# Attention values laid out as [high | low]: two products per part, halves added in SBUF

## The chip, the cores and the metric

The kernel runs on one core of a Trainium2 chip. The metric is the device time of one execution in microseconds. Engines are named as in the profile: PE is TensorE, DVE is VectorE, ACT is ScalarE, POOL is GpSimd, and SP issues most of the loads.

## The reference

Two layers of a decoder trunk over 256 tokens of width 1024. A layer is a feed-forward half-step, a mixer, and a second feed-forward half-step, each between two RMS norms. The mixer runs three branches on one combined projection and merges them by gates:

```
x = x + 0.5 * rms_norm(swiglu(rms_norm(x), w_in, w_out))          # ffn1, ffn2 alike
u, bg, cg, q, kv, nsa_g, q_mem, merge_g = split(h @ w_in)         # mixer
y_conv = bg * short_conv(cg * u, conv_w)                          # width 3
y_nsa  = g0 * (compressed) + g1 * (selected blocks) + g2 * (window)   # 8 heads of 64 in 2 groups
y_mem  = softmax(q_m k_m) v_m                                     # 256 memory tokens, 4 heads of 128
merged = sum_i sigmoid(G_i) * (y_i @ w_branch_i);  x = x + rms_norm(merged @ w_out)
```

The sparse attention ("nsa") has three parts. The compressed part attends to blocks of 32 tokens, each made into one key and one value by a small network with a GELU. With 256 tokens there are four blocks of 64, and all are selected, so the selected part and the window part are both causal attention over all tokens, with keys and values of their own. Each head's three outputs are weighted by gates of the token.

## The kernel before

The 256 tokens are two streams of 128 (t = 0 and 1). Values are kept in fp32 and multiplied as pairs: each operand is split into a high half, a cast to fp32r (on ACT), and a low half, the remainder (a subtraction on DVE), and a product is three matmuls, high by high, low by high and high by low (`mm3`, L336). Weights come by DMA from SP as `raw` tiles of 128x1024 (four buffers, RAWBUFS), and `split_unit` (L276) makes `whi` on ACT and `wlo` on DVE from them (eight buffers each, WBUFS).

The Python program is a loop of steps. A stream yields after each piece of a product; `later(n, fn)` (L326) puts work off by n steps; `background` (L1165) runs up to four lanes of attention tasks beside the streams' products, and new tasks of the kinds "nsa" and "memory" start at least nine steps apart (PACE). The program runs once dry, which records when each weight is asked for, and once for real. Each engine then works through its own list in order; SP's list is that of the loads. The order in the lists, with the waits for data and for free buffers, is all that sets the time.

PSUM has six banks for products (`bank`, L151) and two for transposes (`tbank`, L154). Tiles of 128x520 in SBUF (`ttile`) share eight buffers (TBUFS).

In the mixer of a stream (L1184) the columns of the projection come in this order: keys and values (`kv_first` L692, `kv_second` L735), queries (`q_part` L762), memory queries, the convolution's u, c and b (`conv_part` L1104, `conv_out` L1132), then the gates and branches. Evacuated pieces are turned by TensorE transposes some steps later, which `later` decides: the rotated keys `kd` after three steps (L760), the queries `qe` after two and four, the convolution's input `v` and its gate `bs` after two.

Attention: probabilities `p` go through a turn by DVE (`blocks`), two DMAs on POOL's queue and a split into `turnhi` and `turnlo`, and `attend_values` (L819) multiplies them with the values. The values `vz` of a stream hold, for each kind and group, 128 columns for the high half and 128 for the low one, in which the group's 64 columns are filled and the others are zero; so both groups add up in one bank `o` per stream (`accumulate`, L884), three products per part, and the compressed attention (`cmp_attention`, L1000) adds its product to the same bank. The chain of a bank is closed after three parts (t = 0) or five (t = 1), CHAINS, and then evacuated and split into `ynsa`. The compressed attention is queued as the last of the "nsa" tasks.

Of the kernel before, what the change touches and what calls it, by code (L numbers as in the profile page):

```python
# [28 lines left out]
P = 128  # L29
# [27 lines left out]
CMP = 4  # L57
ATT_A, ATT_B, ATT_C, ATT_D, ATT_T = 1, 3, 2, 5, 10
CHAINS = 3, 5
EARLY, RAMP, SCALES, STAGED = 6, 10, 5, 8  # L60
# [71 lines left out]
def program(tc, nc, pools, a, out, plan):  # L132
# [29 lines left out]


    x = [consts.tile([P, D], F32, name=f"x{t}") for t in range(2)]
    idle = ttile("idle", F32R)
# [377 lines left out]


    dmask = consts.tile([P, P], F32, name="dmask")
    cmadd = consts.tile([P, 2, 16], F32, name="cmadd")
# [5 lines left out]
    smallT = consts.tile([P, 96], F32, name="smallT")  # L552
    vz = [consts.tile([P, 1024], F32R, name=f"vz{t}") for t in range(2)]

    def setup():
# [15 lines left out]
        nc.vector.tensor_reduce(gmask, view(bmask, 0, [[1, 2], [2, 4]]), axis=AX.X, op=OP.add)  # L571
        for t in range(2):
            nc.gpsimd.memset(f32(vz[t]), 0.0)

# [48 lines left out]
    def begin_layer(l):  # L623
        if l == 0:
            with tc.issue_after(latest[0].ins):
                setup()
        S = shared[l] = {"ymem": None, "ynsa": [None] * 2, "o": [None] * 2, "parts": [0, 0],
                         "om": [None] * 2, "mparts": 0, "KC": None,
                         "kd": [None] * 2, "gt": [None] * 2, "QT": [None] * 2, "qm": [None] * 2}
        add(("mem", l), memory(l))  # L630
# [61 lines left out]
    def kv_first(t, l, ps, r):  # L692
        S = shared[l]
        if t == 0:
            S["G"] = [ttile(f"G{i}") for i in range(2)]
            S["KT"] = (gtile("KTh", F32R), gtile("KTl", F32R))
        kvs = ttile("kvs")
        v = kvs[:, 0:384].rearrange("p (x c) -> p x c", x=2)
        src = ps[:, 0:256].rearrange("p (x c) -> p x c", x=2)
        nc.scalar.activation(v[:, :, 0:128], src, AF.Copy, scale=r[0])  # L700
        nc.vector.tensor_scalar(v[:, :, 128:192], src[:, :, 0:64], r[0], None, op0=OP.mult)
        kd = ttile("kd")
        S["kd"][t] = kd
        dup_in(kd, 0, ps, 256, r)
        vpad(t, 0, ps, 384, r)

        def turn():
            pt = tbank()
            for i in range(2):
                nc.tensor.transpose(pt[:, i * 256:i * 256 + P], kvs[:, i * 192:i * 192 + 128], ident)  # L710
                nc.tensor.transpose(pt[:, i * 256 + P:i * 256 + 2 * P], kvs[:, i * 192 + 64:i * 192 + 192], ident)
            for i in range(2):
                G = S["G"][i]
                for half in range(2):
                    col = t * P + 1 - half
                    pr = slice(64 * half, 64 * half + 64)
                    for g in range(2):
                        which = g if half == 0 else 1 - g
                        eng = nc.scalar.copy
                        eng(G[pr, g * 260 + col:g * 260 + col + P],  # L720
                            pt[pr, i * 256 + which * P:i * 256 + (which + 1) * P])

        later(2, turn)
# [5 lines left out]
    def vpad(t, var, ps, c0, r):  # L729
        hi = view(vz[t], var * 512, [[192, 2], [1, 64]])  # L730
        lo = view(vz[t], var * 512 + 256, [[192, 2], [1, 64]])
        src = view(ps, c0, [[64, 2], [1, 64]])
        evac_split(hi, lo, src, r[0])

    def kv_second(t, l, ps, r):  # L735
# [23 lines left out]

        later(3, turn)  # L760

    def q_part(t, l, ps, r):  # L762
# [31 lines left out]

        later(2, turn(0))
        later(4, turn(1))

    def recip_gate(sums, n, gate):
# [5 lines left out]
        return r  # L804

    def values(t, var, g):
        c = var * 512 + g * 128
        return vz[t][:, c:c + 128], vz[t][:, c + 256:c + 384]

# [8 lines left out]

    def attend_values(t, l, parts):  # L819

        def put(hi, lo):
            def go():
                for n, (half, kt, var, g) in enumerate(parts):
                    ph, pl = [v[:, half * 512:(half + 1) * 512] for v in (hi, lo)]
                    c = var * 512 + g * 128
# [3 lines left out]
        return put  # L829

    def nsa_first(l, g):
# [25 lines left out]
        yield ATT_C  # L857
        turn_beside(p, 1024, attend_values(0, l, [(var, 0, var, g) for var in range(2)]), ATT_T)

    def nsa_second(l, var, g):  # L860
# [20 lines left out]
        yield ATT_C  # L881
        turn_beside(p, 1024, attend_values(1, l, [(kt, kt, var, g) for kt in range(2)]), ATT_T)

    def accumulate(t, l, share, products):  # L884
        S = shared[l]
        first = S["o"][t] is None
        if first:
            S["o"][t] = bank("o")
        o = S["o"][t]
        S["parts"][t] += share  # L890
        closing = S["parts"][t] == CHAINS[t]
        for n, (st, mv) in enumerate(products):
            nc.tensor.matmul(o, lhsT=st, rhs=mv, start=(first and (n == 0)),  # L893
                             stop=(closing and n == len(products) - 1), skip_group_check=True)
        if closing:
            y = gtile("ynsa", F32R)
            evac_split(y[:, 0:512], y[:, 512:1024], o)
            S["ynsa"][t] = y

    def compress(l, i):  # L900
# [20 lines left out]
        for u in range(4):  # L921
# [8 lines left out]
            yield 1  # L930
        zc = ttile("zc")
        nc.scalar.copy(zc[0:64, 0:256], z[0:64, 0:256])
        yield 1
        zt = tbank()
        for ht in range(2):
            nc.tensor.transpose(zt[:, ht * 64:(ht + 1) * 64], zc[0:64, ht * P:(ht + 1) * P], ident[0:64, 0:64])
        zv = zt[:, 0:128].rearrange("p (h n) -> p h n", h=2)
        zs = sp.tile([P, 2, 32], F32, name="zs")
# [30 lines left out]
        else:  # L969
# [27 lines left out]
            for tt in range(2):  # L997
                add(("nsa", l, tt), cmp_attention(tt, l))

    def cmp_attention(t, l):  # L1000
# [22 lines left out]
        nc.scalar.copy(view(pc, 32, [[96, 4], [32, 2], [1, 32]]), view(pc, 0, [[96, 4], [0, 2], [1, 32]]))  # L1023
        yield ATT_B
        pt = tbank()
# [5 lines left out]
        yield ATT_D  # L1031
        accumulate(t, l, 1, [(S["VST"][0:96], ph[0:96, :512])])

# [70 lines left out]
    def conv_part(t, l, u_s, c_ps, r):  # L1104
# [23 lines left out]

        later(2, turn)
        return cT  # L1130

    def conv_out(cT, b_ps, r, put):  # L1132
        bs = ttile("bs")
        nc.scalar.activation(bs[:, :512], b_ps, AF.Copy, scale=r[0])

        def turn():
            pt = transpose4(bs, 0)
            nc.vector.tensor_tensor(cT[:, :512], cT[:, :512], pt, op=OP.mult)
            y = gtile("yconv", F32R)
# [4 lines left out]
        later(2, turn)  # L1144

# [183 lines left out]
```

## Time and profile before

| | us |
|---|---|
| runs of the kernel | 1270.59, 1272.78, 1275.57; median 1272.78 |
| profiled execution | 1271.95 |
| span of its trace | 1270.2 |
| PE busy, DVE busy, ACT busy, POOL busy | 1255.8, 895.3, 723.0, 204.3 |

The span is that of the trace; the execution's own time has 1.75 us around it. Busy times of PE are made of printed durations that overlap: a product of 128x512 prints 0.39 us and the next one starts 0.23 us after it. A row of the timeline is: start, duration, engine, line, operation, output <- inputs, and in brackets the idle time before it and what ended that.

### The profile page before, as it was taken

To read this page: it belongs to the slowest core of one execution; us is meant where nothing else is said; L and a number is where in the kernel's file an instruction comes from. 1 tells how busy PE (TensorE), PEld (TensorE's weight loads), DVE (VectorE), ACT (ScalarE), POOL (GpSimd) and SP (SyncE) were. 2 spreads that over 40 slices of the span, in tenths; PEclk is the share of its full clock that TensorE was granted. 3 is DMA by queue.
4 is the path that set the end of the run, shared out by engine and by line. 5 is a ranking of instruction groups with operands and counts; after the bars stand their busy time and mean duration, and the time that the engine had idled before them with its cause. 6 is when DMAs were issued, how large, how long until landed. Compare 5 with 4: busy or idle time off the path is not lost.

```text
span 1270.2 us, 16756 instructions
## 1 busy us (share of the span) xinstructions
PE 1255.8 (99%) x5866; PEld 1037.8 (82%) x5866; DVE 895.3 (70%) x1136; ACT 723.0 (57%) x1123; POOL 204.3 (16%) x404
## 2 busy tenths in 40 slices
PE   9999999999999999999999999999999999999998
PEld 6888888888888788888888888878888888888886
DVE  7767657778887676676576676677798766766753
ACT  5545545877775564454464545568778654545441
POOL 3001600302210010111011013013022100110110
PEclk9999999999999999999999999999999999999999
DMA  7878875776876657787757788748587757577772
GB/s 252 261 246 254 283 255 163 221 229 197 254 247 198 198 170 216 246 262 225 249 174 233 227 269 299 238 146 247 170 259 243 216 178 232 177 233 226 244 249 80
DMA packets 133220, 284.77 MB, mean 224 GB/s; under 512 B 11696, under 2 KB 30800, under 8 KB 133136
## 3 DMA queue, kind: packets, MB, share of 16 engines
q1 hardware_dynamic: 118256, 239.30, 60.4%
q0 software_dynamic: 14848, 44.39, 10.9%
q8 instruction: 46, 0.75, 0.2%
q14 instruction: 38, 0.31, 0.1%
q10 hardware_dynamic: 32, 0.01, 0.0%
HBM read 260.59 MB, written 23.07 MB: 223 GB/s over the span
## 4 chain that ended last, share of the span: by engine, by line
PE 89%; ACT 4%; DVE 3%; DMA 2%; issue 2%; POOL 1%; DVEq 0%; POOLq 0%; ACTq 0%
PE acc L349 34%; PE acc L339 8%; PE acc L337 8%; PE acc L338 8%; PE y L339 7%; PE y L338 7%; PE y L337 7%; PE pt L381 2%; PE br L337 2%; PE br L339 2%; PE br L338 2%; PE o L893 1%; ACT whi L281 1%; DVE wlo L282 1%; DMA raw<-in_cmp_v_w_dram 1%
## 5 line engine op out<-in xcount | busy, mean ns | idle before, releaser
L282 DVE TENSOR_TENSOR wlo<-raw,whi 128x1024 fp32r<-128x1024 f32 (+1 forms) x440 | 532.4, 1214 | 265.4 <-ACT whi L281 261.1
L281 ACT CAST whi<-raw 128x1024 fp32r<-128x1024 f32 (+1 forms) x440 | 458.3, 1046 | 380.2 <-PE acc L349 175.5
L349 PE MATMUL acc<-wlo,hThi 128*128 128x512 f32 x640 | 198.6, 390 | 0.1
L349 PE MATMUL acc<-whi,hThi 128*128 128x512 f32 x640 | 197.7, 390 | 0.8 <-ACT whi L281 0.8
L349 PE MATMUL acc<-whi,hTlo 128*128 128x512 f32 x640 | 197.2, 389 | 0.0
L337 PE MATMUL acc<-whi,hThi 128*128 128x512 f32 (+1 forms) x480 | 187.5, 391 | 0.4 <-ACT hThi L455 0.4
L338 PE MATMUL acc<-wlo,hThi 128*128 128x512 f32 (+1 forms) x480 | 184.9, 385 | 0.0
L339 PE MATMUL acc<-whi,hTlo 128*128 128x512 f32 (+1 forms) x480 | 184.7, 385 | 0.2
L396 POOL DMA_DIRECT2D there<-blocks x176 | 97.0, 557 | 431.7 <-DVE blocks L391 393.0
L349 PEld LDWEIGHTS acc<-wlo,hThi 128*128 128x128 f32 x640 | 120.0, 188 | 25.7 <-DVE wlo L282 0.9
L349 PEld LDWEIGHTS acc<-whi,hThi 128*128 128x128 f32 x640 | 119.6, 188 | 26.1 <-ACT whi L281 1.2
L349 PEld LDWEIGHTS acc<-whi,hTlo 128*128 128x128 f32 x640 | 120.0, 188 | 25.4 <-DVE hTlo L456 0.4
L339 PE MATMUL y<-whi,turnlo 128*128 128x512 f32 x352 | 137.3, 390 | 0.0
L338 PE MATMUL y<-wlo,turnhi 128*128 128x512 f32 x352 | 137.3, 390 | 0.0
L337 PE MATMUL y<-whi,turnhi 128*128 128x512 f32 x352 | 137.1, 389 | 0.0
L339 PEld LDWEIGHTS acc<-whi,hTlo 128*128 128x128 f32 x480 | 90.1, 188 | 18.4 <-DVE hTlo L456 0.6
L337 PEld LDWEIGHTS acc<-whi,hThi 128*128 128x128 f32 x480 | 90.3, 188 | 17.2 <-ACT hThi L455 1.3
L338 PEld LDWEIGHTS acc<-wlo,hThi 128*128 128x128 f32 x480 | 90.4, 188 | 15.3
L337 PEld LDWEIGHTS y<-whi,turnhi 128*128 128x128 f32 x352 | 66.1, 188 | 13.7
L339 PEld LDWEIGHTS y<-whi,turnlo 128*128 128x128 f32 x352 | 66.1, 188 | 13.7
L338 PEld LDWEIGHTS y<-wlo,turnhi 128*128 128x128 f32 x352 | 66.1, 188 | 13.6
L432 POOL TENSOR_TENSOR nr<-nv,mhalf 128x1 f32<-128x1 f32 x28 | 16.7, 597 | 358.0 <-DVE nv L429 357.6
(297 smaller groups left out, 1485.9 us busy)
## 6 DMA issues: line engine op xcount, KB each, us to landing
raw<-in_ffn_w_in_dram SPq DMA_DIRECT2D x160, 512.0 KB, 4.9
raw<-in_w_mix_in_dram SPq DMA_DIRECT2D x96, 512.0 KB, 4.5
raw<-in_ffn_w_out_dram SPq DMA_DIRECT2D x88, 512.0 KB, 4.5
there<-blocks POOLq DMA_DIRECT2D x144, 128.0 KB, 4.3
moved<-there POOLq DMA_DIRECT2D x36, 512.0 KB, 5.5
raw<-in_ffn_w_in_dram SPq DMA_DIRECT2D x32, 256.0 KB, 4.2
raw<-in_w_mem_kv_dram SPq DMA_DIRECT2D x16, 512.0 KB, 4.8
raw<-in_w_mix_out_dram SPq DMA_DIRECT2D x16, 512.0 KB, 4.4
```

The source lines that it names most:

```text
L281: pinned(nc.scalar.copy(hi[:, :n], raw[:, :n]))
L282: pinned(nc.vector.tensor_sub(lo[:, :n], raw[:, :n], f32(hi[:, :n])))
L337: nc.tensor.matmul(ps, lhsT=xh, rhs=wh, start=start, stop=False, skip_group_check=skip)
L338: nc.tensor.matmul(ps, lhsT=xh, rhs=wl, start=False, stop=False, skip_group_check=skip)
L339: nc.tensor.matmul(ps, lhsT=xl, rhs=wh, start=False, stop=stop, skip_group_check=skip)
L349: pinned(nc.tensor.matmul(p[:, :n], lhsT=hT[x2][:, k], rhs=w[:, j * n:(j + 1) * n], start=(k == 0 and i == 0), stop=(k == 7 and i == 2)))
L381: pinned(nc.tensor.transpose(pt[:, j * P:(j + 1) * P], src[:, c0 + j * P:c0 + (j + 1) * P], ident))
L396: nc.gpsimd.dma_start(there[:, q * f:(q + 1) * f].rearrange("(p j) f -> j p f", j=32), blocks[q * 32:(q + 1) * 32, :n].rearrange("j (p f) ...
L432: nc.gpsimd.tensor_tensor(r, v, mhalf, op=OP.pow)
L893: nc.tensor.matmul(o, lhsT=st, rhs=mv, start=(first and (n == 0)), stop=(closing and n == len(products) - 1), skip_group_check=True)
```

## The change

The values of a group become 128 columns, [high | low], 64 each. One product of the high probabilities with all 128 columns gives high by high in the bank's upper 64 rows and high by low in its lower 64; a second one, with the 64 high columns, adds low by high to the upper rows. The halves, the groups and the compressed part are then added in an SBUF tile `yf` by `gather`: ACT copies the compressed part's bank `oc`, DVE adds each half of each group's bank `o`. The compressed attention is queued first and without the pace of nine steps, its transposes two steps later. Apart from that, turns are put off: kd from 3 steps to 5, qe from 2 and 4 to 3 and 5, v and bs from 2 to 3, the product ATT_D from 5 to 6. The keys `kvs` are written by one ACT copy with duplicates, transposed by `transpose4` and copied by four ACT instructions a stream instead of eight. `zc` becomes a constant tile whose transposes are 128x128. In the diff below, the first change of a `later` is that of kd in `kv_second`, the pair that of `q_part`, and the last one stands twice, in `conv_part` and `conv_out`.

```
-        v = kvs[:, 0:384].rearrange("p (x c) -> p x c", x=2)
-        src = ps[:, 0:256].rearrange("p (x c) -> p x c", x=2)
-        nc.scalar.activation(v[:, :, 0:128], src, AF.Copy, scale=r[0])
-        nc.vector.tensor_scalar(v[:, :, 128:192], src[:, :, 0:64], r[0], None, op0=OP.mult)
+        nc.scalar.activation(view(kvs, 0, [[128, 4], [64, 2], [1, 64]]), view(ps, 0, [[64, 4], [0, 2], [1, 64]]),
+                             AF.Copy, scale=r[0])
...
-        later(3, turn)
+        later(5, turn)
...
-        later(2, turn(0))
-        later(4, turn(1))
+        later(3, turn(0))
+        later(5, turn(1))
...
-                for n, (half, kt, var, g) in enumerate(parts):
+                for n, (half, kt, var) in enumerate(parts):
                     ph, pl = [v[:, half * 512:(half + 1) * 512] for v in (hi, lo)]
-                    c = var * 512 + g * 128
-                    vh, vl = vz[kt][:, c:c + 128], vz[kt][:, c + 256:c + 384]
-                    accumulate(t, l, 1 / len(parts), [(vh, ph), (vh, pl), (vl, ph)])
+                    c = var * 256 + g * 128
+                    nc.tensor.matmul(o, lhsT=vz[kt][:, c:c + 128], rhs=ph, start=(count == len(parts) and n == 0),
+                                     stop=False, skip_group_check=True)
+                    nc.tensor.matmul(o[0:64], lhsT=vz[kt][:, c:c + 64], rhs=pl, start=False,
+                                     stop=(closing and n == len(parts) - 1), skip_group_check=True)
+                if closing:
+                    gather(t, l, [(64 * g, 64, o, 0), (64 * g, 64, o, 64)])
...
+    def gather(t, l, sums):
+        for to, n, ps, at in sums:
+            dst, src = yf[to:to + n, :512], ps[at:at + n]
...
+            if not rows & have:
+                nc.scalar.copy(dst, src)
+            elif rows <= have:
+                nc.vector.tensor_tensor(dst, src, dst, op=OP.add)
...
+        S["parts"][t] += 1
+        if S["parts"][t] == 3:
+            y = gtile("ynsa", F32R)
+            nc.scalar.copy(y[:, 0:512], yf[:, :512])
+            nc.vector.tensor_sub(y[:, 512:1024], yf[:, :512], f32(y[:, 0:512]))
+            later(2, lambda: S["ynsa"].__setitem__(t, y))
...
-                add(("nsa", l, tt), cmp_attention(tt, l))
+                add(("cmp", l), cmp_attention(tt, l), True)
...
-        accumulate(t, l, 1, [(S["VST"][0:96], ph[0:96, :512])])
+        o = bank("oc")
+        nc.tensor.matmul(o, lhsT=S["VST"][0:96], rhs=ph[0:96, :512], start=True, stop=True)
+        gather(t, l, [(0, P, o, 0)])
...
-        later(2, turn)
+        later(3, turn)
```

How it moves instructions is shown at three places of layer 0. In TensorE's list before, the first transposes of the rotated keys `kd` (L381) follow the six products of 512 columns that come after the projection's pieces of 280 columns:

```order
L338 MATMUL acc<-wlo,hThi 128x512
L339 MATMUL acc<-whi,hTlo 128x512
L337 MATMUL acc<-whi,hThi 128x512
L338 MATMUL acc<-wlo,hThi 128x512
L339 MATMUL acc<-whi,hTlo 128x512
L381 MATMUL pt<-ident,kd 128x128 x4
L337 MATMUL acc<-whi,hThi 128x280
L338 MATMUL acc<-wlo,hThi 128x280
L339 MATMUL acc<-whi,hTlo 128x280
```

and now, at the same place of TensorE's list:

```order
L337 MATMUL acc<-whi,hThi 128x280
L338 MATMUL acc<-wlo,hThi 128x280
L339 MATMUL acc<-whi,hTlo 128x280
L337 MATMUL acc<-whi,hThi 128x512
L338 MATMUL acc<-wlo,hThi 128x512
L339 MATMUL acc<-whi,hTlo 128x512
L337 MATMUL acc<-whi,hThi 128x512
L338 MATMUL acc<-wlo,hThi 128x512
L339 MATMUL acc<-whi,hTlo 128x512
L381 MATMUL pt<-ident,kd 128x128 x4
L337 MATMUL acc<-whi,hThi 128x512
```

The transposes moved behind the next group of six pieces of 280 columns and six of 512.

The second place is TensorE's list at the first products of probabilities and values (stream 0, first group); `s` are scores, `pc` and `phc` the compressed part's probabilities before and after their transposes. Before:

```order
L841 MATMUL s<-KTh,QT_2337 128x256
L841 MATMUL s<-KTl,QT_2337 128x256
L893 MATMUL o<-turnhi,vz_122 128x512
L893 MATMUL o<-turnlo,vz_122 128x512
L893 MATMUL o<-turnhi,vz_122 128x512 x2
L893 MATMUL o<-turnlo,vz_122 128x512
L893 MATMUL o<-turnhi,vz_122 128x512
L337 MATMUL acc<-whi,hThi 128x512
```

and now:

```order
L381 MATMUL pt<-ident,v 128x128 x4
L1038 MATMUL pt<-ident,pc 96x128 x4
L1044 MATMUL oc<-phc,vst 128x512
L820 MATMUL o<-turnhi,vz_86 128x512
L822 MATMUL o<-turnlo,vz_86 64x512
L820 MATMUL o<-turnhi,vz_86 128x512
L822 MATMUL o<-turnlo,vz_86 64x512
L337 MATMUL acc<-whi,hThi 128x512
```

Six products became four, and the compressed part's transposes and product, which stood some hundred pieces further down, now stand ahead of them.

The third place is DVE's list around stream 0's `v`, the convolution's input c * u (L1107 before, L1120 now); `sc`, `smc` and `pc` belong to the compressed softmax, `rm`, `pm` and `nmm` to the memory attention. Before:

```order
L391 STREAM_TRANSPOSE blocks<-p 128x1024
L1068 TENSOR_SCALAR nmm<-nmm 128x2
L282 TENSOR_TENSOR wlo<-raw,whi 128x1024
L1107 SCALAR_TENSOR_TENSOR v<-acc,rs,us 128x512
L1075 RECIPROCAL rm<-sumsm 128x4
L282 TENSOR_TENSOR wlo<-raw,whi 128x1024 x2
L1067 TENSOR_REDUCE nmm<-sm 128x2
L282 TENSOR_TENSOR wlo<-raw,whi 128x1024
```

and now the last twelve rows up to `v` (two more `wlo` stand above them):

```order
L282 TENSOR_TENSOR wlo<-raw,whi 128x1024
L1029 TENSOR_REDUCE smc<-sc 128x8
L1021 TENSOR_TENSOR sc<-sc,cmadd 128x128
L790 TENSOR_SCALAR rg_2890<-smc 128x8
L1088 RECIPROCAL rm<-sumsm 128x4
L1022 TENSOR_TENSOR sc<-sc 128x128
L791 RECIPROCAL rg_2890<-rg_2890 128x8
L1024 TENSOR_REDUCE nmc<-sc 128x8
L793 TENSOR_TENSOR rg_2890<-rg_2890,gt 128x8
L282 TENSOR_TENSOR wlo<-raw,whi 128x1024
L1032 TENSOR_TENSOR pc<-sc,rg_2890 128x4x32
L1120 SCALAR_TENSOR_TENSOR v<-acc,rs,us 128x512
```

Four `wlo`, the first stream's compressed softmax and a part of the second's came in ahead of `v`.

## Rows read from the trace of the kernel before

**Rows 1.** The page: busy time, share of the span and instructions of an engine, and TensorE's granted clock in 40 slices, in tenths of full speed.

```profile
PE 1255.8 (99%) x5866; PEld 1037.8 (82%) x5866; DVE 895.3 (70%) x1136; ACT 723.0 (57%) x1123; POOL 204.3 (16%) x404
...
PEclk9999999999999999999999999999999999999999
```

**Rows 2.** Windows of 25 us: busy time and number of instructions of PE, PEld, DVE, ACT and POOL, then the granted clock, the DMA engines' share and GB/s.

```profile
50.00:75.00 25.00, 25.00 (x112) 20.71 (x111) 17.76 (x17) 12.32 (x14) 5.63 (x10) 1.00 0.85 265
75.00:100.00 25.00, 25.00 (x112) 20.68 (x111) 17.79 (x18) 11.72 (x12) 1.02 (x2) 1.00 0.71 214
```

**Rows 3.** TensorE's waits: what waited, for what: us in total, how often, the longest.

```profile
PE pt L381 <- POOL kd L750: 2.0, 2, 1.0
...
PE pt L787 <- DVE zs L942: 0.8, 2, 0.6
...
PE s L871 <- DVE gth L1244: 0.7, 1, 0.7
...
PE pt L381 <- ACT bs L1134: 0.4, 1, 0.4
```

**Rows 4.** TensorE's timeline before the keys' transposes of layer 0 and layer 1, and two products of the compression.

```profile
235.27 0.29 PE L338 MATMUL acc<-wlo,hThi 128*128 128x280 f32 x1
235.40 0.29 PE L339 MATMUL acc<-whi,hTlo 128*128 128x280 f32 x1
...
236.45 0.39 PE L338 MATMUL acc<-wlo,hThi 128*128 128x512 f32 x1
236.68 0.39 PE L339 MATMUL acc<-whi,hTlo 128*128 128x512 f32 x1
238.09 0.66 PE L381 MATMUL pt<-ident,kd 128*128 128x128 f32 x4 [1.03 <-POOL kd L750]
...
254.89 0.28 PE L928 MATMUL z<-wlo,FHL 128*32 128x256 f32 x1
255.00 0.28 PE L926 MATMUL z<-whi,FHL 128*64 128x256 f32 x1
255.12 0.28 PE L928 MATMUL z<-wlo,FHL 128*32 128x256 f32 x1
...
864.26 0.39 PE L339 MATMUL acc<-whi,hTlo 128*128 128x512 f32 x1
865.65 0.66 PE L381 MATMUL pt<-ident,kd 128*128 128x128 f32 x4 [1.00 <-POOL kd L750]
```

**Rows 5.** Groups of instructions by line and shape, the products of probabilities and values: busy us, mean ns of one, idle before.

```profile
L893 PE MATMUL o<-turnhi,vz 128*128 128x512 f32 x48 | 17.3, 395 | 0.0
...
L893 PE MATMUL o<-turnlo,vz 128*128 128x512 f32 x24 | 9.7, 403 | 0.0
```

**Rows 6.** POOL's timeline, the last two instructions of the first keys' rope.

```profile
236.35 1.68 POOL L750 TENSOR_TENSOR kd<-ra,rb 128x64 f32<-128x64 f32 x2
```

**Rows 7.** DVE's timeline, stream 0's v in layer 0.

```profile
292.93 1.23 DVE L282 TENSOR_TENSOR wlo<-raw,whi 128x1024 fp32r<-128x1024 f32 x1 [0.77 <-ACT whi L281]
294.07 0.74 DVE L1107 SCALAR_TENSOR_TENSOR v<-acc,rs,us 128x512 f32<-128x512 f32 x1
```

**Rows 8.** TensorE's timeline: the transposes of stream 0's v in both layers, and the eight small products of the compressed scores with the product that follows them.

```profile
298.24 0.60 PE L381 MATMUL pt<-ident,v 128*128 128x128 f32 x4
...
387.25 0.96 PE L1005 MATMUL sc<-kc,QT 128*128 128x32 f32 x8
388.06 0.47 PE L337 MATMUL acc<-whi,hThi 128*128 128x512 f32 x1
...
925.47 0.60 PE L381 MATMUL pt<-ident,v 128*128 128x128 f32 x4
```

**Rows 9.** The chain of waits (start, us, what): the raw load ahead of the cast at 299.59.

```profile
294.19 5.33 DMA raw<-in_w_mix_in_dram
```

**Rows 10.** ACT's timeline behind that load in layer 0, and at the same place in layer 1.

```profile
299.59 1.05 ACT L281 CAST whi<-raw 128x1024 fp32r<-128x1024 f32 x1 [1.35 <-DMA raw<-in_w_mix_in_dram]
300.55 0.58 ACT L1118 COPY vT<-pt 128x512 f32<-128x512 f32 x1
...
926.21 1.05 ACT L281 CAST whi<-raw 128x1024 fp32r<-128x1024 f32 x1 [1.07 <-DMA raw<-in_w_mix_in_dram]
```

**Rows 11.** DVE's timeline of the compressed attention of stream 0, and the two kinds of evacuation by DVE of 512 columns from PSUM.

```profile
391.96 0.28 DVE L1016 TENSOR_TENSOR sc<-sc,cm 128x128 f32<-128x128 f32 x1
...
393.24 0.29 DVE L1021 TENSOR_TENSOR pc<-sc,rg 128x128 f32<-128x128 f32 x1
...
397.27 0.68 DVE L1030 TENSOR_TENSOR phc<-pt,phc 32x512 fp32r<-32x512 f32 x1
...
404.75 0.68 DVE L373 TENSOR_TENSOR ynsa<-o,ynsa 128x512 fp32r<-128x512 f32 x1
```

**Rows 12.** Windows of 5 us over 285 to 330, columns as in rows 2; the last line is the sum of all nine.

```profile
310.00:315.00 5.00, 4.63 (x25) 3.64 (x24) 5.00 (x17) 4.21 (x8) 0.61 (x1) 1.00 0.91 291
315.00:320.00 5.00, 5.00 (x26) 4.13 (x25) 5.00 (x8) 3.65 (x12) 2.19 (x4) 1.00 0.76 207
...
sum 45.00, PE 44.63 PEld 37.51 DVE 39.37 ACT 37.37 POOL 9.06; mean PE 4.96 PEld 4.17 DVE 4.37 ACT 4.15 POOL 1.01
```

More of the change, by code (lines that the diff above doesn't have):

```diff
@@ L161, in ttile @@
         return tp.tile([P, 520], dt, name=name, tag="tmp")
+    vz = [consts.tile([P, 512], F32R, name=f"vz{t}") for t in range(2)]
     x = [consts.tile([P, D], F32, name=f"x{t}") for t in range(2)]
@@ L552, in program @@
     smallT = consts.tile([P, 96], F32, name="smallT")
-    vz = [consts.tile([P, 1024], F32R, name=f"vz{t}") for t in range(2)]
     def setup():
@@ L571, in setup @@
         nc.vector.tensor_reduce(gmask, view(bmask, 0, [[1, 2], [2, 4]]), axis=AX.X, op=OP.add)
-        for t in range(2):
-            nc.gpsimd.memset(f32(vz[t]), 0.0)
+        nc.gpsimd.memset(zc, 0.0)
         posi = consts.tile([P, 2], I32, name="posi")
@@ L626, in begin_layer @@
                 setup()
-        S = shared[l] = {"ymem": None, "ynsa": [None] * 2, "o": [None] * 2, "parts": [0, 0],
+        S = shared[l] = {"ymem": None, "ynsa": [None] * 2, "yf": [None] * 2, "o": [[(None, 0)] * 2 for _ in range(2)], "parts": [0, 0],
                          "om": [None] * 2, "mparts": 0, "KC": None,
@@ L707, in turn @@
         def turn():
[L708 to L711, printed above, removed]
+            pt = transpose4(kvs, 0)
             for i in range(2):
@@ L714, in turn @@
                 for half in range(2):
-                    col = t * P + 1 - half
                     pr = slice(64 * half, 64 * half + 64)
[L717 to L721, printed above, removed]
+                    nc.scalar.copy(view(G[pr], t * P + 1 - half, [[260, 2], [1, P]]),
+                                   view(pt[pr], i * 256, [[P, 2], [1, P]]))
         later(2, turn)
@@ L828, in put @@
             later(ATT_D, go)
         return put
+    def gather(t, l, sums):
+        S = shared[l]
+        if S["yf"][t] is None:
+            S["yf"][t] = (ttile("yf"), set())
+        yf, have = S["yf"][t]
+        for to, n, ps, at in sums:
+            dst, src = yf[to:to + n, :512], ps[at:at + n]
+            rows = {r for r in (0, 64) if to <= r < to + n}
+            if not rows & have:
+                nc.scalar.copy(dst, src)
+            elif rows <= have:
+                nc.vector.tensor_tensor(dst, src, dst, op=OP.add)
+            else:
+                for r in rows:
+                    gather_rows(yf, r, ps, have)
+            have |= rows
+        S["parts"][t] += 1
[4 more added lines that the diff above has]
+            later(2, lambda: S["ynsa"].__setitem__(t, y))
@@ L831, in nsa_first, with gather_rows @@
+    def gather_rows(yf, r, ps, have):
+        dst, src = yf[r:r + 64, :512], ps[r:r + 64]
+        if r in have:
+            nc.vector.tensor_tensor(dst, src, dst, op=OP.add)
+        else:
+            nc.scalar.copy(dst, src)
     def nsa_first(l, g):
@@ L857, in nsa_first @@
         yield ATT_C
-        turn_beside(p, 1024, attend_values(0, l, [(var, 0, var, g) for var in range(2)]), ATT_T)
+        turn_beside(p, 1024, attend_values(0, l, g, [(var, 0, var) for var in range(2)]), ATT_T)
     def nsa_second(l, var, g):
@@ L881, in nsa_second @@
         yield ATT_C
[L882 to L898, printed above, removed]
+        turn_beside(p, 1024, attend_values(1, l, g, [(kt, kt, var) for kt in range(2)]), ATT_T)
     def compress(l, i):
@@ L930, in compress @@
             yield 1
-        zc = ttile("zc")
-        nc.scalar.copy(zc[0:64, 0:256], z[0:64, 0:256])
+        nc.scalar.copy(zc[0:64], z[0:64, 0:256])
         yield 1
@@ L1142, in turn @@
             put(y)
-        later(2, turn)
+        later(3, turn)
     def branch(yT, name, l, n0):
```

26 lines of the change are left out of this document (15 added, 11 removed).

## The prediction

> **What bounds the kernel now.** I read the page's engine shares first: TensorE is busy 1255.8 of 1270.2 us (99%), DVE 70%, ACT 57%, and the granted clock stands at 9 tenths or more in every slice, which is the 2.4 GHz level throughout [rows 1]. A busy TensorE need not be a full one, so next I read the windows of 25 us: in a plain stretch of the first feed-forward it issues 112 products in 25 us, that is one in 0.223 us [rows 2], and the timeline shows the same pace start to start, 236.68 after 236.45, 0.23 us (I use 0.227), for products of 128x512 whose rows print 0.39 us [rows 4]. The printed length is latency; the pace is the price. TensorE goes through its list in order and nearly without a hole, so the time after is the time before, minus the pace of each product that goes, minus each wait that goes, plus each wait that comes. The view of TensorE's waits gives the second: POOL's rope of the keys 2.0 us in two waits, zs 0.8 in two, gth 0.7 in one, bs 0.4 in one [rows 3]. Everything else (DVE, ACT, POOL, DMA) counts only where it makes TensorE wait.
>
> **Products removed.** Three products of 128x512 per part become two, of which the second has 64 instead of 128 weight columns: o<-turnhi falls from 48 to 24, o<-turnlo stays at 24 [rows 5]. So 24 issues go, 24 x 0.227 = 5.45 us. The narrow product is not cheaper: the two products of the compression, with 32 and with 64 weight columns and 256 moving ones, start 0.11 and 0.12 us after each other (254.89, 255.00) [rows 4], as 128x256 ones do, so the moving columns set the pace and 512 of them stay 0.227. The 8 transposes of zc become 128x128 instead of 128x64: same count, at most some hundredths each, nothing.
>
> **Waits removed.** The keys' transposes start at 238.09 where the product before them started at 236.68: 1.41 minus the pace 0.23 is 1.18 us lost; in layer 1 865.65 minus 864.26 minus 0.23 is 1.16 [rows 4]. They wait for POOL's kd, two instructions from 236.35 that take 1.68 together, so until 238.03 [rows 6]. In the new order six products of 280 columns (0.13 us each by 235.27 and 235.40 [rows 4]) and six of 512 come between (the pieces of TensorE's order around these transposes show where they stand): 0.78 + 1.36 = 2.14 us of work, more than 1.18. Both waits go: -2.35. The waits on zs (0.8) and bs (0.4) go because q's and conv's turns come a step later and what they wait for does not; the wait on gth (0.7) is for a bank, and banks are handed out in another order, so I count half. Together -0.8 - 0.4 - 0.35 = -1.55. Bounds: none of these 1.55 (the same bank order turned up elsewhere) to all 1.9.
>
> **What DVE and ACT get.** The compressed attention moves from the mixer's end to its front third. On DVE its ten small operations, of which cm (391.96) to pc (393.24) are six in 1.57 us, and phc with 0.68 [rows 11], come to about 2.5 + 0.68 for each of the two streams, 6.4 us a layer. New on DVE are 16 additions yf of 64x512. Before has none; 32x512 from PSUM took 0.68 and 128x512 took 0.68 [rows 11], so the partitions don't matter and each is 0.68, 10.9 us in all, four of a layer in the crowded stretch. ACT gets four copies of 128x512 and loses 16 copies of the keys, DVE loses four scalings. None of that is on the path by itself: the split weights have eight buffers each (WBUFS), so a cast or a wlo that is 1 or 2 us late need not be missed. What can't give way is a small tile that TensorE wants soon, and DVE works through its list in order.
>
> **The wait that may come: v.** In the pieces of DVE's order, v (conv's input) stands in before right behind one wlo: wlo 292.93, v 294.07, done 294.81 [rows 7]. TensorE's transposes of v come at 298.24 [rows 8], 3.4 us later. In the new order four more wlo and most of the compressed softmax stand ahead of v, and the last wlo needs the cast whi that in before ran at 299.59, having waited 1.35 us for a raw load that was issued at 294.19 and took 5.33 [rows 9, 10]. That cast ends at 300.64; wlo adds 1.23, pc 0.29 less some overlap, v 0.74: v is ready at about 302.8. TensorE comes to these transposes later too: between the transposes of zc and those of v there are 17 more 128x512 products, two groups of eight small ones of 32 columns (0.81 us a group, 387.25 to the next start at 388.06 [rows 8]) and 6 fewer of 128x256 (0.117) in the new order: 3.86 + 1.62 - 0.70 = 4.8 us, so at 303.0. No wait, with 0.2 to spare. In layer 1 the transposes stood at 925.47 [rows 8], now 19 more products, 5.2 us, 930.7; the last wlo ahead of v needs the whi of 926.21 [rows 10], 927.26, wlo to 928.49, then nine small operations at some 0.25 (2.3), v: 931.5. Wait: 0.8. What goes earlier (kd, zs) moves both sides alike, since the raw load hangs on DVE and ACT, which are fed by TensorE's scores. The transposes of pc follow one product behind those of v and need pc's copy on ACT, behind the scalings of pm there; I add 0.3 a layer. Sum +1.4. Bounds 0 (the load a little earlier) and 4.5: 1.2 more in each layer if one more wlo, or a cast in front of pc's copy (1.05), comes between, and 0.35 twice for the other stream's v.
>
> **Smaller waits that come.** The transposes of qms now stand three products (0.68) behind those of qe instead of six, and share a two-buffer PSUM pool with them: transposes end some 0.28 after their issue and a copy of 128x512 on ACT takes 0.58 [rows 10], 0.86 against 0.68, so 0.2; with a cast of 1.05 in front it would be 1.2. I take 0.3 a layer, +0.6. At the end, ynsa comes over two additions, an ACT copy and a subtraction (4 x 0.68) instead of one split evacuation, put off by two steps, that is by products which cover it: 0.2 a layer, +0.4 (bounds 0 and 1.2 a layer).
>
> **The sum.** -5.45 - 2.35 - 1.55 + 1.4 + 0.6 + 0.4 = -6.95 us. The profiled execution took 1271.95 us (span 1270.2), so 1265.0; from the median of the runs shown, 1272.78, it would be 1265.8. I say 1265.0.
>
> **Rivals.**
> A: the added waits don't come (the raw load lands earlier, or the queues give DVE slack that my bookkeeping in before's clock doesn't see). For it: DVE's v had 3.4 us to spare. Then -9.35: 1262.6.
> B: DVE falls behind once in each layer. In the nine windows of 285 to 330 DVE is busy 39.37 of 45 us, and 5.00 of 5 in two of those shown [rows 12]; 5.6 us are free. Into that stretch go 6.4 + 4 x 0.68 = 9.1 us, so it ends some 3.5 us behind. If TensorE meets all of it, 7.0 instead of my 1.4: -1.35, 1270.6.
> C, slower: DVE's free time can't be used, since its holes are waits for scores, casts and loads that move along with it; then the whole 9.1 us come out at whatever of v, phc, turnlo, bs or the yf additions holds the next PSUM bank, 18.2 over two layers, and TensorE loses 18.2 - 9.35 = +8.85: 1280.8. It decides from where DVE's lag is above about 8 us a layer (more than +6.4 in all). Against it: the weights' low halves, over half of DVE's work there, have slack to give. The Trainium skill, in "Trainium Kernel Development and Optimization", Best Practices, says to mind PSUM pressure: making TensorE cheaper does nothing for emptying PSUM. Here emptying even grows, four evacuations of o become four copies and sixteen additions; by that rule the case is C, and by the rows, which show no wait of TensorE on o's evacuation at all [rows 3], it is not; no run here has shown it yet.
> D: the narrow product is cheaper than 0.227, by the printed length of weight loads or in proportion to its columns: at half the price 24 x 0.114 = 2.7 more, 1262.3. The pace of the 32- and 64-column products [rows 4] speaks against it.
> E: the wait for kd only moves, to whatever needs the keys next (scores a step later): the 2.35 are not won, 1267.4.
>
> **Chances.** My sum (1262.8 to 1267.2) 0.45; A, below that, 0.13; B, between that and C's foot, 0.18; C 0.09; D 0.05; E 0.10. What counts as a difference here is 0.5%, 6.4 us, so below 1266.4 is faster and above 1279.1 slower. Of my sum's range 1262.8 to 1266.4 is four fifths, but my errors lean to the late side (a wait forgotten is likelier than one invented), so I count 0.32 of the 0.45 as faster; with A, D and 0.02 of E that is 0.52. Slower: C and 0.01 of B, 0.10. The rest, 0.38, is the same. For 8 in 10 the range has to reach to A on one side and over E and most of B on the other: 1261 to 1274. The likeliest case's own range is 1262.8 to 1267.2.
>
> **What the profile after will show.** TensorE's rows o<-turnhi x24 and o<-turnlo x24 with starts 0.23 apart, for the second kind too (else D). No wait on POOL kd in the view of waits (else E), none on zs and bs. New entries there: pt <- DVE v or the ACT copy of pc, about 1 us in layer 1 and less in layer 0 (none: A; 3 us or more in a layer, or entries on phc, oc, yf: B or C). DVE's five-us windows after the start of the compressed softmax full up to the end of that stretch, and the 16 additions at 0.68. I am wrong on the mechanism, not only in size, if the gain or loss lies outside the two mixer stretches, for in the feed-forwards nothing is changed, or if TensorE's clock leaves its level.

## The result

In the comparison that came with the change, the kernel after took 1266.53 us (median of 4 runs, 1265.63 to 1267.51), the kernel before 1272.72 (4 runs): ratio 0.995, interval [0.9929, 0.9971]. Two later comparisons, on two chips, gave 0.9928 [0.9903, 0.9952] and 0.9945 [0.9924, 0.9967]. One of the eight executions of the last one took 4068.67 us, at a granted clock of 0.30, and stands in no median or ratio here. The prediction was 1265.0 (1261 to 1274). The profiled execution took 1266.82 us, span 1265.1.

The page of the kernel after answers to [rows 1]: TensorE has 24 instructions less and is as full as before.

```profile
PE 1250.5 (99%) x5842; PEld 1033.9 (82%) x5842; DVE 901.8 (71%) x1148; ACT 723.7 (57%) x1111; POOL 199.3 (16%) x403
```

The groups by line and shape answer to [rows 5]; the last one is the new work of DVE.

```profile
L840 DVE TENSOR_TENSOR yf<-o,yf 64x512 f32<-64x512 f32 x16 | 11.0, 685 | 0.4
L820 PE MATMUL o<-turnhi,vz 128*128 128x512 f32 x24 | 9.5, 396 | 0.0
L822 PE MATMUL o<-turnlo,vz 128*64 128x512 f32 x24 | 9.5, 395 | 0.5 <-DVE turnlo L417 0.5
```

TensorE's waits answer to [rows 3] (us in total, how often, the longest):

```profile
PE br L337 <- ACT ynsa L848: 2.3, 1, 2.3
...
PE o L822 <- DVE turnlo L417: 0.5, 1, 0.5
...
PE pt L381 <- DVE v L1120: 0.4, 1, 0.4
PE pt L381 <- ACT QT L779: 0.3, 1, 0.3
```

All four waits of [rows 3] are gone, and a new one of 2.3 us stands at the top. Its price is more than that. Behind it, the granted clock falls (windows of 5 us, columns as in [rows 2]):

```profile
405.00:410.00 5.00, 4.61 (x21) 3.35 (x19) 4.90 (x6) 2.27 (x3) 0.00 (x0) 1.00 0.78 234
410.00:415.00 5.00, 3.08 (x9) 2.35 (x10) 1.88 (x3) 0.78 (x2) 0.00 (x0) 0.76 0.58 185
415.00:420.00 5.00, 5.00 (x21) 4.09 (x20) 3.97 (x5) 2.99 (x4) 0.00 (x0) 0.90 0.33 100
```

Nine products in 5 us where a full window has 22; the wait takes 1.9 us of the window. A mean of 0.76 is a mix of the two levels, 1.2 and 2.4 GHz: soon after the idle stretch seven products of 128x512 follow each other at 0.43 us instead of 0.23. So the order in the lists and the waits are not quite all that sets the time: what follows a long wait can run slower.

**Where the time went.** For a balance I took from each trace, for every shape of matmul, the median from start to start, times its count, and put what a product took above that down to the wait in front of it. The paces add up to 1243.99 us before and 1238.38 after; what stands above them to 18.61 and 19.08.

| after minus before, profiled executions | us |
|---|---|
| products (sum of paces) | -5.61 |
| waits that went: kd -2.35, zs -1.05, gth -0.83, bs -0.54, zc -0.18 | -4.95 |
| ynsa: wait +2.71 (2.48 in layer 0, 0.23 in layer 1), lower clock behind it +1.40 | +4.11 |
| other new waits: turnlo 0.68, v 0.52, qms 0.44, KTl 0.28, pc 0.20 | +2.12 |
| waits under 0.13 us each, the start and the rest | -0.81 |
| first to last product of TensorE (1262.37 to 1257.23) | -5.14 |

The gain lies in the mixers and is uneven. From TensorE's first transposes of x in the mixer to those in the feed-forward behind it, layer 0 took 1.26 us less than before (239.73) and layer 1 took 4.05 less (236.96); the feed-forwards between the two mixers took 386.57 us in both kernels.

### The profile page after: what moved, and what is told of

It is laid out like the page before. It is cut to its first block, busy times and chain, and to the rows that moved or that the text cites. A ratio compares the mean times of both kernels' runs of the same rounds, so it can differ in the third digit from the quotient of the medians.

```text
span 1265.1 us, 16698 instructions
## 1 busy us (share of the span) xinstructions
PE 1250.5 (99%) x5842; PEld 1033.9 (82%) x5842; DVE 901.8 (71%) x1148; ACT 723.7 (57%) x1111; POOL 199.3 (16%) x403
## 4 chain that ended last, share of the span: by engine, by line
PE 90%; DVE 3%; DMA 2%; ACT 2%; issue 2%; POOL 1%; SPq 0%; DVEq 0%; POOLq 0%; ACTq 0%
PE acc L349 34%; PE acc L339 8%; PE acc L337 8%; PE acc L338 8%; PE y L339 7%; PE y L338 7%; PE y L337 7%; PE pt L381 2%; PE br L337 1%; PE br L339 1%; PE br L338 1%; DVE wlo L282 1%; DMA moved<-there 1%; ACT whi L281 1%; DMA x<-in_x_dram 1%
```

## The experiments

Every kernel was compared with the kernel before on its own chip; ratios are to that. Single executions of one kernel lie up to 10 us apart (one source of it is in the last section), so waits are read from the traces and the ratios only where they are far apart. A wait that the text gives from start to start, as in the balance, is some 0.16 us longer than the idle time that the views print for it.

**The delay of the keys alone, in the kernel before** (`kv_second`).

```
-        later(3, turn)
+        later(5, turn)
```

> The kernel before with one number changed: the keys' turn is put off by 5 steps, not 3. Theory 1 (each wait on TensorE is a term of its own): both waits on POOL kd go, 1.18 + 1.16 us, and nothing takes their place, so the time falls by 2.3 us and the view of waits has no kd. Rival (the wait only moves): the scores or the next turn wait instead, the time stays within 0.5 us, and a new entry of some 1 us a layer stands in the view.

Measured: 1272.91 us (before 1274.44), ratio 0.9991 [0.9974, 1.0007]. The waits on kd are gone, but the view of waits has these:

```profile
PE s L871 <- DVE gth L1244: 1.5, 2, 1.1
...
PE acc L337 <- ACT mThi L646: 1.1, 1, 1.1
```

The second is of the memory projection, which the edit does not touch. The first is the rival in part: scores wait for a PSUM bank that DVE's gth has to free, 1.82 us by start to start where before had 0.83. So of the 2.35 us about 1.0 only moved. The time can't tell the two theories apart, for its interval holds both. That the kernel after has no wait on gth is due to its other parts.

**What a product costs.**

```
+                    nc.tensor.matmul(o[0:64], lhsT=vz[kt][:, c:c + 64], rhs=pl, start=False,
+                                     stop=False, skip_group_check=True)
```

> The kernel after with the narrow product of 64 columns issued twice (24 products of 64x512 more; the term high x low is counted twice, so the output differs). Theory 1 (a product costs its pace, whatever its columns): +24 x 0.227 = +5.4 us over the kernel after, that is as slow as before's three products were. Rival (the narrow product is cheap, or such products lie beside waits): +2.7 us or less.

Measured: 1268.53 us, 0.9969 [0.9949, 0.999]. The sum of paces is 1244.04, that is 5.66 above the kernel after: the narrow product costs what a wide one does. The time rose by less, 2 to 5 us by the ratios of the kernel after (0.9928 to 0.995), in part since the wait on ynsa in layer 0 was 1.19 us in this trace and no product behind it ran at the lower level; the rival's half price is not what the paces show.

**Before's delays in the kernel after** (`kv_second`, `q_part`, and the last in `conv_part` and `conv_out`).

```
-        later(5, turn)
+        later(3, turn)
-        later(3, turn(0))
-        later(5, turn(1))
+        later(2, turn(0))
+        later(4, turn(1))
-        later(3, turn)
+        later(2, turn)
```

> The kernel after with before's delays of the turns: kd 3, qe 2 and 4, v 2, bs 2. Theory 1: the waits on kd (2.3 us), zs (0.8 to 1.05) and bs (0.4 to 0.5) come back, +3.5 to +3.9 us over the kernel after, and the wait on v (0.5) grows since its transposes come earlier while DVE's order keeps v behind the compressed softmax. Rival (the delays themselves cost as much as they save, through other waits): within 1 us of the kernel after.

Measured: 1276.18 us, 1.0011 [0.9991, 1.0032]: the whole gain is lost, more than theory 1 said. In its view of waits:

```profile
PE br L337 <- ACT ynsa L848: 3.9, 1, 3.9
PE acc L337 <- ACT mThi L645: 2.8, 1, 2.8
...
PE pt L777 <- DVE zs L953: 1.4, 2, 0.7
...
PE pt L947 <- ACT zc L943: 0.9, 2, 0.7
```

zs (1.69 by start to start) and zc (1.26) came back, kd with 0.62 only, bs and v not. The rest is ynsa with 4.3 and the clock behind such waits, 3.0, about half of it behind mThi, which is not of the change. Without mThi and what followed it, this trace still stands some 5.5 us above the first one of the kernel after; how often the other executions had that wait is not known. All ten took longer (1271.90 to 1281.06) than any of the kernel after counted here (1263.16 to 1270.35, other chips). That the turns' delays change the wait on ynsa 150 us later was in neither theory.

**The layout alone.** Before's delays as above, and:

```
-                add(("cmp", l), cmp_attention(tt, l), True)
+                add(("nsa", l, tt), cmp_attention(tt, l))
-        yield ATT_B + 2
+        yield ATT_B
-ATT_A, ATT_B, ATT_C, ATT_D, ATT_T = 1, 3, 2, 6, 10
+ATT_A, ATT_B, ATT_C, ATT_D, ATT_T = 1, 3, 2, 5, 10
```

> The kernel after with before's delays of all turns, the compressed attention at the end and ATT_D 5: only the layout, the gather and the keys' copies are left of the change. Theory 1 (terms add up): the 24 products go (5.5 us by the sum of paces), the waits on kd, zs and bs stay in part (2 to 3 us), waits on ynsa come (2 to 4 us a layer): within 2 us of the kernel before on this chip. Rival (the layout alone is the gain, the moves are ornament): 5 to 6 us below the kernel before.

Measured: 1266.56 us (before 1272.85), 0.9955 [0.9934, 0.9976]. Seven of its ten executions took 1264.7 to 1267.6. The rival is right: this much of the change wins nearly all. It is not the values' layout alone, though: the keys' copies are in it, and kd, with before's delay, costs 0.61 where before had 2.35; no run separates the two. In its trace zs costs 1.62, kd 0.61, bs 0.47, pc 2.78 (2.35 in one wait of layer 1), and ynsa nothing, which theory 1 had at 4 us or more. By the ratios the kernel is some 7 us faster than the one of the run above, which has the same short delays and differs in the compressed attention's place and steps (ATT_B) and in ATT_D.

**The compressed attention at the end, everything else as in the kernel after** (the first of the three edits above).

> The kernel after with the compressed attention queued as before, as the last of the paced tasks. Theory 1 (its move to the front costs a little on DVE there and takes its DVE work away from the end): the wait on v goes (-0.5), but the compressed bank's gather is then the last one, with three chained evacuations right ahead of the branch (no product between o and ynsa in the first of the two), so waits on ynsa of 2 us or more in both layers: 2 to 5 us over the kernel after. Rival (rival B or C of the prediction, DVE overloaded in the front stretch): 2 us or more below the kernel after.

Measured: 1267.44 us, 0.9943 [0.9923, 0.9963]. The wait on v is gone and ynsa has two of 1.5 us, in both layers as theory 1 said, but under its 2 us:

```profile
PE br L337 <- ACT ynsa L848: 2.7, 2, 1.4
```

The time is the same as the kernel after's within the intervals. So the front place of the compressed attention does not overload DVE by what rival B or C needed, and it is not shown to pay.

**A second and a third trace of the kernel after.**

> The kernel after, unchanged, on the chip of the other three runs of this group and as a second trace. Theory 1 (the wait on ynsa in layer 0 is set by the last turn's DMAs landing in a burst of loads): a wait on ynsa of 1 to 4 us at the same place, some lower clock behind it, turnhi waiting 5 us or more for the DMA, the time 1265 to 1268.5. Rival (a chance event of the first trace): no wait over 0.3 us there, the time about 3.9 us lower.

Measured: 1264.84 us, 0.9928 [0.9903, 0.9952]; the wait on ynsa in layer 0 is 1.90 us by the view (2.06 from start to start), and turnhi waits 5.4 us for its DMA. The lower clock did not come, the granted clock of 410 to 415 us is 1.00 this time, and the time lies just under the range expected.

> The kernel after once more, beside the other three on their chip: 1264 to 1267 us, 0.5 to 0.7% under before; a wait on ynsa of 1.5 to 4 us in layer 0.

Measured: 1266.31 us (median of seven executions; before 1272.40), 0.9945 [0.9924, 0.9967]; two waits on ynsa, 2.9 us in all, the longest 2.1, and a granted clock of 0.66 in the 5 us after the longest. The wait belongs to the place, not to chance.

**Where the wait on ynsa comes from.** In the kernel after, layer 0, TensorE:

```profile
405.58 0.40 PE L820 MATMUL o<-turnhi,vz 128*128 128x512 f32 x1
405.82 0.39 PE L822 MATMUL o<-turnlo,vz 128*64 128x512 f32 x1
411.92 0.50 PE L337 MATMUL br<-whi,ynsa 128*128 128x512 f32 x1 [2.32 <-ACT ynsa L848]
```

DVE at the same place:

```profile
402.36 1.23 DVE L417 TENSOR_TENSOR turnlo<-moved,turnhi 128x1024 fp32r<-128x1024 f32 x1 [5.38 <-ACT turnhi L416]
403.50 3.69 DVE L282 TENSOR_TENSOR wlo<-raw,whi 128x1024 fp32r<-128x1024 f32 x3
407.11 0.68 DVE L1257 SCALAR_TENSOR_TENSOR gth<-gth,br 128x512 f32<-128x512 f32 x1
407.82 0.69 DVE L1258 TENSOR_TENSOR merged<-merged,gth 128x512 f32<-128x512 f32 x1
408.55 0.69 DVE L840 TENSOR_TENSOR yf<-o,yf 64x512 f32<-64x512 f32 x1
409.26 1.23 DVE L282 TENSOR_TENSOR wlo<-raw,whi 128x1024 fp32r<-128x1024 f32 x1
410.52 0.69 DVE L840 TENSOR_TENSOR yf<-o,yf 64x512 f32<-64x512 f32 x1
```

and ACT:

```profile
401.28 1.05 ACT L416 CAST turnhi<-moved 128x1024 fp32r<-128x1024 f32 x1 [5.79 <-DMA moved<-there]
```

o is complete at 406.2, but DVE begins the first addition at 408.55. It had stood still for 5.38 us, because its next instruction was turnlo and the last turn's data had not landed; three wlo and two other operations were queued behind. Then come the two additions with a wlo between them, the cast of ynsa (0.62), and TensorE. The turn's DMAs were issued at 386.29 and 393.43, and the second took 7.8 us to land, in a stretch where the loads of the branch's weights run; in before the same pair went out at 383.24 and 390.14 and the second landed in 4.7.

In layer 1 DVE goes through the same list, a wlo between the two additions included, but it waited 2.59 us at turnlo, not 5.38, and TensorE lost only 0.23 us:

```profile
1026.90 1.22 DVE L417 TENSOR_TENSOR turnlo<-moved,turnhi 128x1024 fp32r<-128x1024 f32 x1 [2.59 <-ACT turnhi L416]
...
1033.63 0.68 DVE L840 TENSOR_TENSOR yf<-o,yf 64x512 f32<-64x512 f32 x1
1034.34 1.23 DVE L282 TENSOR_TENSOR wlo<-raw,whi 128x1024 fp32r<-128x1024 f32 x1
1035.60 0.69 DVE L840 TENSOR_TENSOR yf<-o,yf 64x512 f32<-64x512 f32 x1
```

The three traces of the kernel after give six such places. Where DVE waited 3.84, 4.96, 5.17 and 5.38 us at turnlo, the first addition began 0.80, 1.93, 2.13 and 2.34 us after o's end, 3.04 less each time; where it waited 2.59 and 2.67, the addition began 0.1 us after. So the first 3 us of DVE's wait cost the additions nothing, and what lay above them put the additions off in full.

**One step earlier for the products.** `ATT_D` 6 to 5.

> The kernel after with the products of probabilities and values one step earlier (ATT_D 5), so o closes six products, 1.4 us, sooner and ynsa's branch stands as far behind as before. Theory 1 (DVE is behind its list when o closes, by 2.3 us, since turnhi waited for the last turn's DMA and held ACT's casts): o being earlier doesn't help, the wait on ynsa stays within 0.5 us of the kernel after's in its own run. Rival (the chain from o over two additions and a cast is simply too long for the products in between): the wait falls by 1.4 us.

Measured: 1265.13 us, 0.9937 [0.9912, 0.9962]. ynsa waits 1.30 us in layer 0 and 0.88 in layer 1, 2.2 together where the kernel after beside it had 2.3; turnlo now costs 1.18. In sum as theory 1 said, but not by layer, so this run alone would not decide.

**Attention tasks every 8 steps.**

```
-PACE, PACED = 9, ("nsa", "memory")
+PACE, PACED = 8, ("nsa", "memory")
```

> The kernel after with attention tasks started every 8 steps, not 9, so that the last products of probabilities and values stand some 36 rows further ahead of the branch that needs ynsa. Theory 1: the wait on ynsa in layer 0 (2.3 us idle and 1.4 us of products at the lower clock level behind it) goes, -3.5 to -4 us, granted clock 1.000. Rival (the late turn's DMA and DVE's lag are what costs, and they show up wherever the last turn stands): a wait of 2 us or more on turnhi, turnlo or ynsa remains and the time stays within 1 us.

Measured: 1266.67 us (before 1274.44), 0.9939 [0.9908, 0.997]. No wait on ynsa and turnhi waits 0.6 us, not 5.8, for its DMA: the cause by place holds. The time does not show the gain that theory 1 had, it is that of the kernel after within the intervals, as the rival said of it. About half of the gain is eaten by a new entry, scores that wait for a bank:

```profile
PE s L899 <- DVE merged L1255: 1.9, 1, 1.9
```

**The cast off ACT.**

```
+            if pool:
+                nc.gpsimd.tensor_copy(hv, mv)
+            else:
+                nc.scalar.copy(hv, mv)
...
+        turn_beside(p, 1024, attend_values(1, l, g, [(kt, kt, var) for kt in range(2)]), ATT_T, g == 1 and var == 1)
```

> The kernel after with one cast a layer moved from ACT to POOL: that of turnhi for the last attention task, which waits for the turn's DMA. TensorE's order is the same. Theory 1 (ACT stands still for 5 us at this cast, the casts of the weights behind it are late, and DVE is 2.3 us behind its list when o closes): ACT's wait goes, DVE has little to do when o closes, the first addition starts within 0.8 us of o's end (2.3 in after), and the wait on ynsa in layer 0 falls from about 2 to under 0.5 us: 2 to 3.5 us under the kernel after, unless POOL's cast is so slow (3 us or more) that o waits for turnlo instead. Rival (the chain of two additions and a cast is too long by itself): the wait stays at 1.5 us or more.

Measured: 1265.4 us (before 1272.40), 0.9947 [0.9929, 0.9965]. ACT no longer stands still, but DVE does, at the same instruction (POOL's cast first, then DVE):

```profile
401.23 1.04 POOL L417 CAST turnhi<-moved 128x1024 fp32r<-128x1024 f32 x1 [5.48 <-DMA moved<-there]
```

```profile
402.30 1.23 DVE L420 TENSOR_TENSOR turnlo<-moved,turnhi 128x1024 fp32r<-128x1024 f32 x1 [4.47 <-POOL turnhi L417]
403.44 3.49 DVE L282 TENSOR_TENSOR wlo<-raw,whi 128x1024 fp32r<-128x1024 f32 x3
```

The first addition began at 408.29, 1.2 us after o's end, and ynsa waited 1.36 us, between the two theories. My theory had the engine wrong: what holds up the additions is DVE's own list, in which turnlo stands ahead of three wlo, and not ACT's casts. From turnlo's start to the first addition DVE took 5.99 us here and 6.19 in the kernel after; the 1.2 us are fewer than 2.3 mainly because o closed 0.85 us later. The late DMA as the root fits the traces: in the three of the kernel after, the one with the third product and the one with before's delays, turnhi waits 5.0 to 6.6 us for it and ynsa 1.2 to 4.1 us in layer 0; at 8 steps, turnhi waits 0.6, the first addition begins 0.04 us after o's end, and ynsa does not wait at all, though there the branch also stands further off. That it is late because of the loads beside it was read from the landing times and not tried by itself.

**The parts put together anew.** New delays, but the compressed attention as in the run with the layout alone (end, ATT_D 5, ATT_B).

> The kernel after with the compressed attention at the end as before, ATT_D 5 and its transposes not put off, but with the new delays of kd, qe, v and bs. Theory 1 (terms add up): against the run with the layout alone, the waits on zs (1.6), kd (0.6) and bs (0.5) go; against the kernel after, the wait on ynsa goes and up to 2.8 us on pc in layer 1 may come: 1262 to 1265.5 us, at or up to 2 us under the kernel after. Rival (the front place of the compressed attention is what pays): 2 us or more over the kernel after.

Measured: 1264.2 us, 0.9927 [0.9904, 0.9951], lowest median of its group (kernel after 1266.31). No wait on zs, kd, bs or ynsa; pc costs 1.88, QT 1.42.

> As the run before with attention tasks every 8 steps. Theory 1: twenty products stand between the last o and its branch and the turns' DMAs come earlier, no wait over 1 us on ynsa or pc: 1261 to 1264.5 us, the fastest of all. Rival (the tasks closer together crowd DVE and the banks, as the wait on merged in layer 1 showed at 8 steps with the compressed part in front): a wait of 1.5 us or more on gth or merged, no faster than at 9 steps.

Measured: 1265.72 us, 0.9943 [0.9921, 0.9965]: over theory 1's range and no faster than at 9 steps, as the rival said, but without its wait on gth or merged; instead there are five entries of 0.9 to 1.0 (turnlo twice, pc, p, turnhi). The intervals of these two and of the kernel after overlap, so none is shown to be faster than the kernel after.

## Why the prediction was right

Time, direction and range held: 1265.0 forecast; 1266.53, 1264.84 and 1266.31 measured, 6 to 8 us under before. By the bound of 0.5% that the prediction set itself, the first comparison (0.995, 6.19 us) is on the edge and the two others lie beyond it, with intervals that reach across. By its steps:

- **Products, -5.45:** -5.61 by the paces, and doubling the narrow product gave +5.66. Rival D falls.
- **Waits removed, -2.35 and -1.55:** -2.35 on kd and -2.60 on the others; I had the wait on gth at half and it went altogether, and I took zs and bs as the view prints them, 0.8 and 0.4, where from start to start they cost 1.05 and 0.54. But the reason I gave for kd was not the only one. With before's delay the two waits cost 0.62 in the kernel after and 0.61 with the layout alone, not 2.35 (the reason is in the last section), so the delay won only that. And in the kernel before the same delay moved 1.0 us of them to gth: rival E, in part, and only there.
- **v, 0 in layer 0 and 0.8 in layer 1:** no wait and 0.52. In layer 0 v was ready at 300.99 and TensorE came at 301.73; I had 302.8 and 303.0. The order of DVE's list and the counts of products were enough for that:

```profile
300.25 0.74 DVE L1120 SCALAR_TENSOR_TENSOR v<-acc,rs,us 128x512 f32<-128x512 f32 x1
...
301.73 0.60 PE L381 MATMUL pt<-ident,v 128*128 128x128 f32 x4
```

- **pc 0.3 a layer:** 0.20 in all. **qms 0.3 a layer:** 0.44 in all.
- **ynsa, 0.4:** the step that failed. I worked out its chain as four operations of 0.68, covered by the products in between, with DVE free when o closes. In layer 1 DVE was free, and the chain, with a wlo between the additions that I had left out, took 3.42 us from o's end to the end of the cast; fifteen products of 0.227 us cover that, and the wait was 0.23. In layer 0 DVE was 2.3 us behind its list, since the last turn's data came late, and the wait of 2.48 drew 1.40 of lower clock: 3.9 us, half of the forecast gain. The bound I had set, 1.2 a layer, was too small, because it left out how late the engine itself can be and that TensorE can pay for a long wait twice. TensorE's clock leaving its level was one of my own signs of a wrong mechanism; it left it here, at this term.
- **Rivals B and C**, a DVE that falls behind in the front stretch, did not come. DVE is full there, and TensorE hardly notices: 0.2 us on pc in layer 0, 0.52 on v in layer 1. Five-us windows of the kernel after, as in [rows 12]:

```profile
295.00:300.00 5.00, 5.00 (x28) 4.27 (x27) 4.94 (x14) 2.86 (x7) 0.69 (x2) 1.00 0.91 262
300.00:305.00 5.00, 5.00 (x31) 4.30 (x30) 5.00 (x13) 2.64 (x6) 2.56 (x5) 1.00 0.95 356
305.00:310.00 5.00, 5.00 (x26) 4.22 (x26) 4.96 (x15) 3.06 (x3) 0.10 (x1) 1.00 0.66 225
```

  That the weights' halves gave way, as the prediction said against C, fits these rows; no run tried it by itself. Emptying PSUM did cost TensorE something once: at the end, where two additions in a row stand between the last product and its user, and there DVE's lag was most of it.

The total came out close because the waits that went were worth 1.05 more than I had counted and small ones fell, while ynsa cost 3.7 more. That part of the closeness is luck; the terms for the products and for kd, and the small ones for v and qms, came within 0.3 us each.

## What to carry to other kernels

Where TensorE is full, count products by their start-to-start pace and waits one by one; such a sum came within 2 us in 1270 here, with errors of 1 and 3.7 us in it that partly cancelled. The term to fear is a chain at the end of a branch with nothing behind it: ask not only how long its operations are but how far behind its list the engine will be when the chain begins, and what that engine's list has waiting for a DMA just ahead. Moving work to another place has to be tried with the delays that go with it: the front place of the compressed attention, with its later steps and before's delays, cost by the medians all that the layout had won.

## What the runs showed of the hardware

**POOL beside DVE.** The two kd instructions of POOL took 1.68 us in before [rows 6]. In the kernel after they are the same instructions:

```profile
236.37 0.93 POOL L740 TENSOR_TENSOR kd<-ra,rb 128x64 f32<-128x64 f32 x2
```

In before DVE had a wlo, a subtraction of two SBUF operands, from 236.56 to 237.86 beside them, and they ended at 238.03:

```profile
236.56 1.30 DVE L282 TENSOR_TENSOR wlo<-raw,whi 128x1024 fp32r<-128x1024 f32 x1
```

In after the DVE operations there are two shorter products F, until 237.15, and they ended at 237.30:

```profile
236.03 1.12 DVE L924 TENSOR_TENSOR F<-G,smallT 128x240 f32<-128x240 f32 x2
```

Over all eight their mean is 0.88 us before and 0.44 after. The Trainium skill, in "SBUF — State Buffer", section "Who interferes with whom", has it that a DVE instruction with two SBUF inputs contends with a GpSimd instruction that reads SBUF, and that the pair of ports they share is an exclusive lock; both traces agree, with POOL's second instruction ending some 0.15 us behind DVE's operation. Beside KTl, whose first input is in PSUM, the last of the eight in the kernel after took 0.32 us and ended first. With before's delay and the rest of the change, the two instructions take 0.92 us as well and kd costs 0.62. So 1.73 of the 2.35 us of kd went with DVE's order, which I had not counted on, and not with the delay.

**The clock after a wait.** After 2.32 us of idle TensorE (kernel after) and after 2.11 (its third trace), the granted clock fell to the lower level for the next few us; after 1.90 (its second trace) and 1.20 (the cast on POOL) it stayed. The length of one wait is not all that decides: with the keys' delay alone it fell after waits of 1.13 and 0.53 us that lie 1.3 us apart. The seven slow products in the first case cost 1.40 us.

**The scatter of single executions.** In five of the twelve traces of these runs, TensorE waits for mThi, a cast of the memory tokens' turn, near 177 us or near 801 us, between 0.8 and 3.1 us, four times with the lower clock behind. No edit touches that part. In the run with the layout alone it is the first entry of the view, and that execution took 1271.13 us where the median is 1266.56:

```profile
PE acc L337 <- ACT mThi L645: 3.1, 1, 3.1
```
